# Attention logits: the product with the low part of k is given all 128 rows

## The chip, the cores and the metric

The kernel runs on one core of one Trainium2 chip. The metric is the device time of one execution in microseconds (us); lower is better. Differences of up to about 0.2% can't be told from no change with the measurements of this kernel.

## The reference, cut to what matters

The program is one block of a first network (gated linear attention, called GLA below, beside softmax attention) and two layers of a second one (softmax attention with a forget gate beside retention), all on 512 tokens of width 1024. The softmax attention of the second network, per head of 64 columns:

```
scores = jnp.einsum('bqhd,bkhd->bhqk', q_i, k).astype(jnp.float32) * scale
bias = c_i[..., :, None] - c[..., None, :]
logits = jnp.where(causal, scores + bias, -jnp.inf)
p = jax.nn.softmax(logits, axis=-1)
return jnp.einsum('bhqk,bkhd->bqhd', p.astype(v.dtype), v)
```

The first block does the same with normalized q and k and a bias by distance. Each of the three attention stages has 8 heads.

## The kernel before, in words

**Numbers in two parts.** Most matrix products run on operands of type fp32r, in which a number is held as a high part and a low part (the rest). A product of two numbers is then three products on TensorE: high with high, high with low, low with high. Activations are tiles of 128 partitions by 512 tokens; the weights come in blocks of 128x1024 through the queue of SyncE, ScalarE makes the high part of a block (wh) and VectorE the low part (wl).

**Two heads at a time.** `attention_pair` takes a PSUM tile of q and one of k, features on the partitions: head 2i on partitions 0 to 63 (in the code `r` for hh = 0), head 2i+1 on 64 to 127. For each head it makes a tile `qs`, whose half `r` is the high part of q and whose other half `x` is the low part, and a tile `kh` with the high part of k on both halves. One product over 128 partitions, `qs` with `kh`, so sums high q with high k and low q with high k. A second product on the half `r` alone, of 64 partitions, adds high q with low k (tile `kl`, shared by the two heads, one half each). The low part with the low part is left out.

**Logits.** They go by query tile t = 3, 2, 1, 0 of 128 tokens, with 512, 384 and 256 key columns (t = 1 and t = 0 share a PSUM tile of two times 256). So a head has four pairs of products, kh and then kl. VectorE adds the bias and takes the minimum (tiles ea, eb, ec, and mx for the minima), ScalarE does the exponential, VectorE scales, TensorE transposes, copies go to pta, ptb, ptc, and eight products with v give the output y of the pair, split in two by ScalarE (ymh, in the second network mixh) and VectorE (yml, mixl).

**What sets the order.** A planner in the kernel (`Weave`) interleaves threads into one order of TensorE's instructions. It holds an estimated time of TensorE and of the other engines; a thread goes on when its estimated inputs are there and PSUM banks are free by the estimate. Its cost of a product goes by the columns, not by the rows. PSUM has four banks for projections (tiles `mm`) and four for all else (tiles `at`), each taken in turn, and a product waits until the last reader of its bank is done. The order of ScalarE, VectorE and the queues is found by a scheduler when the program is built. On the chip each engine runs its own order and waits on semaphores. Projections, which have much work and need no result of the attention, fill TensorE between the steps of attention.

Names in the rows: `mm<-wh,xTh` is a projection, `at<-kh,qs` and `at<-kl,qs` the two products of the logits (first the moving operand, then the stationary one), `at<-g,u` a product of the GLA gate with 96 rows, z and cum its decays. In rows of instruction order the numbers tell tiles apart.

Of the kernel before, what the change touches and what calls it, by code (L numbers as in the profile page):

```python
# [10 lines left out]
F32 = mybir.dt.float32  # L11
# [21 lines left out]
# ---------------------------------------------------------------- weight order  # L33
def _blocks():
    """Keys (array, layer, k0, k1, c0, c1, kind) of the weight blocks."""
    out = []

    def a(name, l, c0, n, k=D, w=P):
        out.extend((name, l, 0, k, c, c + w, "") for c in range(c0, c0 + n, w))

    def b(name, l, k0, k1, c0):
        out.extend((name, l, k, k + 2 * P, c0, c0 + 512, "") for k in range(k0, k1, 2 * P))

    def low(name, l, c0, n):
        out.append((name, l, 0, D, c0, c0 + n, "low"))

    for c in (0, 512, 1024):
        b("w_in", 0, 0, D, c)
    low("w_in", 0, 3584, 16)
    a("w_in", 0, 1536, 1024)  # L50
    b("w_in", 0, 0, D, 2560)
    b("w_in", 0, 0, D, 3072)
    b("w_in", 0, 0, D, 3600)
    b("w_in", 0, 0, D, 4112)
    for i in range(4):
        for j in range(2):
            a("w_in", 0, 4624 + (2 * i + j) * P, P)
            a("w_in", 0, 5648 + (2 * i + j) * P, P)
        a("w_branch_moba", 0, 256 * i, 256, 512, 256)
        a("w_branch_gla", 0, 256 * i, 256)  # L60
    for n in range(2):
        b("w_out", 0, 0, D, 512 * n)

    def ffn(up, down, l):
        for h in range(2):
            a(up, l, 2048 * h, 2048)
            for n in range(2):
                b(down, l, 2048 * h, 2048 * (h + 1), 512 * n)

    ffn("w_up", "w_down", 0)  # L70
    for l in range(2):
        a("w_in_2", l, 0, 1024)
        low("w_in_2", l, 1536, 8)
        b("w_in_2", l, 0, D, 1024)
        a("w_in_2", l, 1544, 1024)
        b("w_in_2", l, 0, D, 2568)
        a("w_in_2", l, 3080, 512)
        for n in range(2):
            b("w_out_2", l, 0, D, 512 * n)
        ffn("w_ff1_2", "w_ff2_2", l)  # L80
    return out
# [16 lines left out]
# ---------------------------------------------------------------- constants  # L98
# [38 lines left out]
# columns of the array of per-partition vectors  # L137
# [16 lines left out]
class Event:  # L154
    """A point in the estimated time of the tensor engine."""

    t = None


class Weave:  # L160
    """Interleaves generators into one order of instructions for the tensor engine. A generator
    yields 0 to go on, or (n, event): until the event, or without one until the estimated end of
    what it gave to other engines, and until n banks of PSUM are free."""
# [10 lines left out]
    def fork(self):  # L174
        """What follows doesn't depend on the thread's earlier work on other engines."""
        self.chain = self.now
# [9 lines left out]
    def bank(self, tile):  # L186
        """A new tile takes the bank that is free first."""
        del self.banks[min(self.banks, key=self.banks.get)]
        self.banks[tile.tensor.name] = self.now
# [4 lines left out]
    def done(self):  # L194
        """The end of what the thread has given to other engines since it went on."""
        ev = Event()
        ev.t = self.ready + LAG
        return ev
# [34 lines left out]
class Engine:  # L233
    """An engine whose instructions are charged to the weave's estimate."""
# [4 lines left out]
    def book(self, start, cost):  # L239
        """The end of an instruction in the first gap from start on."""  # L240
        self.busy = [b for b in self.busy if b[1] > self.wv.now]
        t = start
        for a, b in self.busy:
            if t + cost <= a:
                break
            t = max(t, b)
        self.busy = sorted([*self.busy, (t, t + cost)])
        return t + cost
# [19 lines left out]
def model_kernel(ctx: ExitStack, tc: tile.TileContext, I, out):  # L268
# [59 lines left out]
    def split2(hi, lo, x, scale=None):  # L328
        """hi and lo of scale * x."""
        if scale is None:  # L330
            copy(hi, x)
            sub_lo(lo, x, hi)
        else:
            act.activation(hi, x, AF.Copy if isinstance(scale, float) else AF.Identity, scale=scale)
            dve.scalar_tensor_tensor(lo, x, scale, hi.bitcast(F32), ALU.mult, ALU.subtract)

    # ------------------------------------------------------------ weights
# [6 lines left out]
    def load(dst, src):  # L344
        """A load that must not run far ahead: queued behind the newest weights."""
        with tc.issue_after(last_dma[0].ins):
            nc.sync.dma_start(dst, src)
# [23 lines left out]
    class Acts:  # L371
        """K-chunks of [128, 512] as hi and lo, in groups of four or one by one."""
# [12 lines left out]
        def split(self, k, x, scale=None):  # L385
            """Chunk k = x, or scale * x with a column."""
            split2(self.hs[k], self.ls[k], x, scale)
            wv.mark(self.ev[k])

    def form_a(ps, w, c, acts, ks, toks=slice(0, T)):  # L390
        """ps[f, tok] = w[:, :, c:c+128]^T acts."""
# [9 lines left out]
    def form_b(ps, ws, acts, ks, t, first, last):  # L401
        """ps[tok, 512] += acts[:, t]^T w over blocks of two chunks."""
# [15 lines left out]
    def proj_b(name, l, k0, k1, c, acts, done, koff=0, tail=0, wait_k=False, wait_t=False, pre=None):  # L418
        """done(t, ps) as a token tile ends. The last `tail` chunks go token tile by token tile;
        pre(k) makes chunk k of acts."""  # L420
# [21 lines left out]
    # ------------------------------------------------------------ constants  # L442
# [20 lines left out]
    def rstd_col(dst, var, scale, eps):  # L463
        """dst = (var * scale + eps) ** -0.5 of up to 8 columns."""
        pool.tensor_scalar(dst, var, scale, eps, ALU.mult, ALU.add)
        pool.tensor_tensor(dst, dst, mhalf[:, 0 : dst.free_size()], ALU.pow)

    def rstd_tile(st, scale, eps, out=None):
        """(st * scale + eps) ** -0.5 of a [128, 512] PSUM tile, one Newton step after exp(-ln/2)."""
# [16 lines left out]
    def sigmoid(s, x):  # L486
        """s = 1 / (1 + exp(-x)) as exp(-ln(1 + exp(-x)))."""
        act.activation(s, x, AF.Exp, scale=-1.0)
        act.activation(s, s, AF.Ln, bias=one)
        act.activation(s, s, AF.Exp, scale=-1.0)  # L490

    def log_sigmoid(dst, t, a):
        """dst = min(t, 0) - ln(1 + exp(-|t|)); a is room."""
# [5 lines left out]
    def row_bcast(src, n0):  # L499
        """[128, 512] tile, every partition with src[n0 : n0 + 512] of a DRAM vector."""  # L500
# [4 lines left out]
    # ------------------------------------------------------------ attention with softmax  # L505
    def attention_pair(i, operands, v, bias, acts_out, done=None):
        """Softmax attention of heads 2i and 2i + 1. operands() -> PSUM tiles of q and k, [128, 512]
        feature-major, and their scales, q's negated; v[t]: [128, 512] token-major; bias(h) ->
        function t -> pieces (a, b, tile) added to the negated logits; the result goes to acts_out's
        chunk i as hi and lo."""  # L510
        qps, kps, qscale, kscale = yield from operands()
        room, ops, klo = [], [], bt("kl", F32R)
        for hh in range(2):
# [3 lines left out]
            qs, kh = bt("qs", F32R), bt("kh", F32R)  # L517
# [4 lines left out]
            ops.append((qs, kh, klo, r, bias(2 * i + hh), wv.done()))  # L522
        ec, pc2 = bt("ec"), bt("ptc")
        for hh in range(2):
            qs, kh, kl, r, pieces, ev = ops[hh]
            # probabilities by query tile t
            ea, eb = bt("ea"), bt("eb")
            es = [eb[:, 384:512], ec[:, 256 * hh : 256 * hh + 256], eb[:, 0:384], ea]
            for t in (3, 2, 1, 0):
                if t:  # L530
                    yield 1, ev
                    sx = at_ps()
                    for u in (t, 0) if t == 1 else (t,):
# [3 lines left out]
                        mm(s[:, :m], qs[r, u * P : u * P + P], kl[r, :m], False, True)  # L537
# [16 lines left out]
        # transposed by key tile  # L554
# [34 lines left out]
    # ------------------------------------------------------------ tails of a block  # L589
    def transpose_split(z, acts, t, n):  # L590
        """z: [128 tok, 512] -> chunks 4n.. of acts at tokens of t."""
# [18 lines left out]
    def add_to(res, n, alpha, part=None, then=None):  # L610
        """For proj_b: res[t][n] = alpha * res[t][n] + ps, then part(t, n) and the thread then(t)."""
# [56 lines left out]
    class LayerNorm:  # L668
        """In place over the two halves of each token tile."""
# [34 lines left out]
    # ================================================================ block 1  # L704
# [23 lines left out]
    def first_norm():  # L728
        """rstd of the first norm, as a tile over tokens and as columns."""
# [13 lines left out]
    def t5_rows():  # L743
        """T5 bias by distance, with the mask, negated, to DRAM; read back shifted by partition."""
# [21 lines left out]
    def qk_norm(dst, evs):  # L766
        """For proj_b: each head's 64 columns over their norm, without the gain."""
# [39 lines left out]
    def low_proj(w, n, acts):  # L807
        """[n, 512] product with the narrow weight columns, in SBUF."""
# [17 lines left out]
    def gla_decay(u2, g2):  # L826
        """Cumulative log decay (times 16) within chunks of 64 tokens."""
# [12 lines left out]
    def gla_head(h, gq, gk):  # L840
# [14 lines left out]
        # within a pair of chunks  # L855
# [16 lines left out]
        # over pairs: decays from the pair's start, and to its end  # L872
# [52 lines left out]
    def block1():  # L925
# [34 lines left out]
        # GLA  # L960
# [38 lines left out]
        # gates, branches  # L999
# [51 lines left out]
    # ================================================================ block 2  # L1051
# [13 lines left out]
    def ret_head(l, i, q, k, vs, decay, xi, zeta, sg, mix):  # L1065
        """Retention by chunks of 128 tokens."""
# [130 lines left out]
# ---------------------------------------------------------------- launch  # L1197
# [39 lines left out]
```

## Time and profile before

| | |
|---|---|
| median of 3 runs | 2110.65 us (2107.73 to 2112.83) |
| span of the profiled execution | 2108.8 us |
| TensorE busy | 2072.4 us, 98% of the span |
| weight loads busy | 1689.5 us, 80% |
| VectorE, ScalarE, GpSimd busy | 45%, 38%, 16% |
| mean granted TensorE clock | 0.994 of full speed |

The span runs from the first to the last instruction of the profiled execution; it lies 1.85 us under the median of the runs. A TensorE instruction is shown with a modelled end and overlaps the next, so that the distance from one start to the next, and not the duration, tells what it costs there.

### The profile page before, as it was taken

The numbers are of one execution on the slowest core, as the hardware profiler recorded it, in microseconds if no ns is written. First come the engines' busy times: TensorE is split into PE (matmuls) and PEld (weight loads), VectorE is DVE, ScalarE is ACT, GpSimd is POOL, SyncE is SP. The second block draws the span as 40 slices with busy tenths as digits, with TensorE's granted clock in tenths as the row PEclk, the third lists the DMA queues.
The fourth block names the chain that finished last, engine by engine and source line by source line (L and its number), as shares of the span: only waits on it lengthen the run. The fifth ranks groups of instructions, "written<-read, shape, count | busy, mean of one in ns | idle before, by whom it ended". The sixth has DMA issues, their size and how long they took to land.

```text
span 2108.8 us, 24494 instructions
## 1 busy us (share of the span) xinstructions
PE 2072.4 (98%) x9694; PEld 1689.5 (80%) x9694; DVE 945.2 (45%) x1602; ACT 797.4 (38%) x1237; POOL 344.0 (16%) x313
## 2 busy tenths in 40 slices
PE   8999999999999999999999999999999999999998
PEld 6777778889888888867888888888767888888886
DVE  6666444444322322475555323324674554323333
ACT  5655344333422431454334322322454334312421
POOL 2000100001300210010513300212111423201202
PEclk9999999999999999999999999999999999999999
DMA  5421112242322222322232222222322233222221
GB/s 194 151 101 60 50 65 96 100 146 81 104 100 92 98 100 80 126 90 71 80 110 90 100 91 99 100 92 78 131 85 77 74 101 104 97 100 97 93 100 40
DMA packets 62370, 202.67 MB, mean 96 GB/s; under 512 B 7278, under 2 KB 7744, under 8 KB 62256
## 3 DMA queue, kind: packets, MB, share of 16 engines
q1 hardware_dynamic: 62256, 201.12, 28.1%
q8 instruction: 76, 1.25, 0.2%
q14 instruction: 38, 0.31, 0.0%
HBM read 198.94 MB, written 4.77 MB: 97 GB/s over the span
## 4 chain that ended last, share of the span: by engine, by line
PE 94%; POOL 2%; DVE 2%; ACT 1%; issue 1%; DMA 0%; SPq 0%; POOLq 0%; ACTq 0%; DVEq 0%
PE mm L310 85%; PE at L310 7%; PE at L319 2%; POOL h L262 1%; POOL mv L262 1%; DVE h L262 0%; ACT h L262 0%; ACT sil L262 0%; DVE wl L262 0%; DMA xr<-in_xT_dram 0%; DVE og L262 0%; DVE bs L262 0%; ACT wh L262 0%; POOL gm L262 0%; DVE qs L262 0%
## 5 line engine op out<-in xcount | busy, mean ns | idle before, releaser
L262 DVE TENSOR_TENSOR wl<-wr,wh 128x1024 fp32r<-128x1024 f32 (+1 forms) x337 | 426.5, 1266 | 655.1 <-ACT wh L262 652.9
L262 ACT ACTIVATE wh<-wr 128x1024 fp32r<-128x1024 f32 (+1 forms) x340 | 358.9, 1057 | 783.1 <-PE mm L310 739.4
L310 PE MATMUL mm<-hTh,wh 128*128 128x512 f32 (+1 forms) x864 | 318.3, 368 | 0.0
L310 PE MATMUL mm<-hTl,wh 128*128 128x512 f32 (+1 forms) x864 | 317.5, 368 | 0.0
L310 PE MATMUL mm<-hTh,wl 128*128 128x512 f32 (+1 forms) x864 | 317.5, 367 | 0.0
L310 PE MATMUL mm<-wh,uh 128*128 128x512 f32 x768 | 299.2, 390 | 0.0
L310 PE MATMUL mm<-wh,ul 128*128 128x512 f32 x768 | 299.0, 389 | 0.0
L310 PE MATMUL mm<-wl,uh 128*128 128x512 f32 x768 | 298.9, 389 | 0.0
L262 POOL TENSOR_TENSOR ub<-ua 128x512 f32<-128x512 f32 x96 | 153.2, 1596 | 643.8 <-ACT ua L262 643.8
L310 PE MATMUL mm<-xTh,wh 128*128 128x512 f32 x536 | 217.9, 407 | 0.0
L310 PE MATMUL mm<-xTl,wh 128*128 128x512 f32 x536 | 209.3, 391 | 0.0
L310 PE MATMUL mm<-xTh,wl 128*128 128x512 f32 x512 | 200.2, 391 | 0.0
L310 PEld LDWEIGHTS mm<-hTh,wh 128*128 128x128 f32 x864 | 165.0, 191 | 26.1
L310 PEld LDWEIGHTS mm<-hTl,wh 128*128 128x128 f32 x864 | 164.9, 191 | 26.1
L310 PEld LDWEIGHTS mm<-hTh,wl 128*128 128x128 f32 x864 | 164.7, 191 | 26.1
L310 PEld LDWEIGHTS mm<-wh,ul 128*128 128x128 f32 x768 | 144.2, 188 | 29.9
L310 PEld LDWEIGHTS mm<-wh,uh 128*128 128x128 f32 x768 | 144.2, 188 | 29.8
L310 PEld LDWEIGHTS mm<-wl,uh 128*128 128x128 f32 x768 | 144.2, 188 | 29.8
L310 PE MATMUL mm<-wh,xTh 128*128 128x512 f32 x352 | 146.3, 416 | 11.5 <-ACT wh L262 6.0
L310 PE MATMUL mm<-wl,xTh 128*128 128x512 f32 x352 | 139.3, 396 | 0.1
L310 PE MATMUL mm<-wh,xTl 128*128 128x512 f32 x352 | 138.8, 394 | 0.5 <-DVE xTl L262 0.5
L262 DVE TENSOR_TENSOR ul<-ub,uh 128x512 fp32r<-128x512 f32 x96 | 66.5, 692 | 153.2 <-ACT uh L262 153.2
(260 smaller groups left out, 2629.2 us busy)
## 6 DMA issues: line engine op xcount, KB each, us to landing
wr<-in_wall_dram SPq DMA_DIRECT2D x338, 512.0 KB, 3.5
row<-cd SPq DMA_DIRECT2D x16, 256.0 KB, 3.8
revp<-rev SPq DMA_DIRECT2D x1, 2560.0 KB
xr<-in_xT_dram SPq DMA_DIRECT2D x8, 256.0 KB, 6.1
g<-revp SPq DMA_DIRECT2D x8, 256.0 KB, 3.9
h<-in_x_dram SPq DMA_DIRECT2D x8, 256.0 KB, 6.0
row<-in_ln_g_dram SPq DMA_DIRECT2D x8, 256.0 KB, 4.7
row<-in_ln_b_dram SPq DMA_DIRECT2D x8, 256.0 KB, 5.7
```

Of the source, the lines that this page charges most:

```text
L262: return f(out, *a, **k)
L310: nc.tensor.matmul(out, lhsT, rhs, start=start, stop=stop)
L319: nc.tensor.transpose(out, in_, ident)
```

## The change

Each head gets a `kl` tile of its own. The half `r` is written as before, and ScalarE copies it to the other half `x`, as it does for `kh`. The second product then runs over all 128 partitions, so it also adds low q with low k. The diff (comments, which it also takes out, are left away):

```diff
-        room, ops, klo = [], [], bt("kl", F32R)
+        room, ops = [], []
...
-            qs, kh = bt("qs", F32R), bt("kh", F32R)
+            qs, kh, klo = bt("qs", F32R), bt("kh", F32R), bt("kl", F32R)
...
             copy(kh[x], kh[r].bitcast(F32))
-            ops.append((qs, kh, klo, r, bias(2 * i + hh), wv.done()))
+            copy(klo[x], klo[r].bitcast(F32))
+            ops.append((qs, kh, klo, bias(2 * i + hh), wv.done()))
...
-            qs, kh, kl, r, pieces, ev = ops[hh]
+            qs, kh, kl, pieces, ev = ops[hh]
...
-                        mm(s[:, :m], qs[r, u * P : u * P + P], kl[r, :m], False, True)
+                        mm(s[:, :m], qs[:, u * P : u * P + P], kl[:, :m], False, True)
```

Since the planner books the new copy, it also puts the products in another order. Two places follow, from the first pair of the first block, and one from a later pair.

ScalarE, first pair of the first block, before: the steps of the first head (qs, kh and the copy of kh), then those of the second, and between them z of the GLA gate.

```order
L262 ACTIVATE qs_158_814<-at_155_803,gains_97 64x512 [waits PE_49]
L262 ACTIVATE kh_159_815<-at_156_804,gains_97 64x512 [waits PE_49]
L262 ACTIVATE kh_159_815<-kh_159_815 64x512 [waits Activation_49]
L262 ACTIVATE qs_161_823<-at_155_803,gains_97 64x512 [waits DVE_49]
L262 ACTIVATE kh_162_824<-at_156_804,gains_97 64x512 [waits DVE_49]
L262 ACTIVATE z_169_838<-at_168_836,cols_81 128x512 [waits PE_49]
L262 ACTIVATE kh_162_824<-kh_162_824 64x512 [waits Activation_49]
L262 ACTIVATE z_172_848<-at_171_846,cols_81 128x512 [waits PE_49]
```

The same place of the change:

```order
L262 ACTIVATE qs_157_813<-at_155_803,gains_97 64x512 [waits PE_49]
L262 ACTIVATE kh_158_814<-at_156_804,gains_97 64x512 [waits PE_49]
L262 ACTIVATE kh_158_814<-kh_158_814 64x512 [waits Activation_49]
L262 ACTIVATE kl_159_815<-kl_159_815 64x512 [waits DVE_49]
L262 ACTIVATE qs_161_824<-at_155_803,gains_97 64x512
L262 ACTIVATE kh_162_825<-at_156_804,gains_97 64x512
L262 ACTIVATE kh_162_825<-kh_162_825 64x512 [waits Activation_49]
L262 ACTIVATE z_170_841<-at_169_839,cols_81 128x512 [waits PE_49]
L262 ACTIVATE kl_163_826<-kl_163_826 64x512 [waits DVE_49]
```

The copy of kl waits for VectorE's kl of the first head and stands ahead of the second head's qs and kh, and so ahead of all that follows them.

TensorE, a little later, the second head of the same pair, before: after its product for t = 3 (not shown) there are 33 products of projections, of which the last six are shown, and then t = 2.

```order
L310 MATMUL mm_201_1006<-xTh_1_87,wh_203_1008 128x512 [waits Activation_49]
L310 MATMUL mm_201_1006<-xTl_3_89,wh_203_1008 128x512
L310 MATMUL mm_201_1006<-xTh_1_87,wl_204_1011 128x512
L310 MATMUL mm_201_1006<-xTh_1_87,wh_203_1008 128x512
L310 MATMUL mm_201_1006<-xTl_3_89,wh_203_1008 128x512
L310 MATMUL mm_201_1006<-xTh_1_87,wl_204_1011 128x512
L310 MATMUL at_205_1019<-kh_162_824,qs_161_823 128x384 [waits DVE_49]
L310 MATMUL at_205_1019<-kl_157_813,qs_161_823 128x384
```

The same head in the change:

```order
L310 MATMUL mm_147_761<-wh_182_901,xTh_2_88 128x512
L310 MATMUL mm_147_761<-wl_183_904,xTh_2_88 128x512
L310 MATMUL mm_147_761<-wh_182_901,xTl_4_90 128x512
L310 MATMUL at_193_963<-kh_162_825,qs_161_824 128x512 [waits Activation_49]
L310 MATMUL at_193_963<-kl_163_826,qs_161_824 128x512
L310 MATMUL at_195_971<-kh_162_825,qs_161_824 128x384 [waits DVE_49]
L310 MATMUL at_195_971<-kl_163_826,qs_161_824 128x384
L310 MATMUL mm_144_758<-wh_198_980,xTh_2_88 128x512
L310 MATMUL mm_144_758<-wl_199_983,xTh_2_88 128x512
```

The 33 products now stand behind t = 2, which is the fifth user of the four banks and so waits until VectorE has read the first head's t = 3.

TensorE, third pair of the first block, in the change (nine products of projections stand between the two parts, left out): the transposes of k for the fourth pair stand right ahead of the third pair's logits. Before, each pair's transposes of q and k stand behind the last transposes of the pair ahead of it.

```order
L319 MATMUL at_314_1465<-ident_91,qn_103_517 128x128
L319 MATMUL at_314_1465<-ident_91,qn_106_537 128x128
L310 MATMUL at_327_1500<-kh_293_1401,qs_292_1400 128x512 [waits DVE_49,PE_49]
L310 MATMUL at_327_1500<-kl_294_1402,qs_292_1400 128x512 [waits Activation_49]
...
L310 MATMUL at_329_1517<-kh_293_1401,qs_292_1400 128x384 [waits DVE_49]
L310 MATMUL at_329_1517<-kl_294_1402,qs_292_1400 128x384
L310 MATMUL at_331_1525<-kh_293_1401,qs_292_1400 128x256 [waits DVE_49,PE_49]
L310 MATMUL at_331_1525<-kl_294_1402,qs_292_1400 128x256
```

The product with 384 columns takes the bank of the second pair's y, and the first one with 256 columns the bank of the fourth pair's q.

## Rows read from the trace of the kernel before

**Rows 1.** The page: head, busy time, and the granted clock in 40 slices.

```profile
span 2108.8 us, 24494 instructions
...
PE 2072.4 (98%) x9694; PEld 1689.5 (80%) x9694; DVE 945.2 (45%) x1602; ACT 797.4 (38%) x1237; POOL 344.0 (16%) x313
...
PEclk9999999999999999999999999999999999999999
```

**Rows 2.** The page: chain that ended last, by engine.

```profile
PE 94%; POOL 2%; DVE 2%; ACT 1%; issue 1%; DMA 0%; SPq 0%; POOLq 0%; ACTq 0%; DVEq 0%
```

**Rows 3.** TensorE's waits: us in total, times, longest us.

```profile
PE mm L310 <- DVE qs L262: 3.4, 2, 1.7
PE at L319 <- DVE og L262: 3.0, 3, 1.6
```

**Rows 4.** Instructions that write or read kl, by form, and idle time before.

```profile
L310 PE MATMUL at<-kl,qs x96: 379/410/502, 95.0 to 1604.0; 64*128 64x256 f32 x48, 64*128 64x512 f32 x24, 64*128 64x384 f32 x24
...
  issue: 14.8, 56
```

**Rows 5.** TensorE in order of time, first logits: start, us, stationary tile, moving operand.

```profile
94.65 0.39 PE L310 MATMUL at<-kh,qs 128*128 128x512 f32 x1
94.97 0.50 PE L310 MATMUL at<-kl,qs 64*128 64x512 f32 x1
95.40 0.50 PE L310 MATMUL mm<-wh,xTh 128*128 128x512 f32 x1
95.73 0.39 PE L310 MATMUL mm<-wl,xTh 128*128 128x512 f32 x1
95.96 0.39 PE L310 MATMUL mm<-wh,xTl 128*128 128x512 f32 x1
96.18 0.33 PE L310 MATMUL at<-kh,qs 128*128 128x384 f32 x1
...
98.40 0.39 PE L310 MATMUL mm<-wl,xTh 128*128 128x512 f32 x1
```

**Rows 6.** TensorE in order of time, up-projection of the first block, 256 columns.

```profile
517.93 0.28 PE L310 MATMUL mm<-hTh,wh 128*128 128x256 f32 x1
518.05 0.28 PE L310 MATMUL mm<-hTl,wh 128*128 128x256 f32 x1
```

**Rows 7.** TensorE in order of time, a product with 96 rows.

```profile
93.73 0.39 PE L310 MATMUL at<-g,u 96*128 96x512 f32 x1
93.97 0.39 PE L310 MATMUL mm<-wh,xTh 128*128 128x512 f32 x1
```

**Rows 8.** ScalarE in order of time, first pair's operands.

```profile
89.61 0.63 ACT L262 ACTIVATE kh<-kh 64x512 fp32r<-64x512 f32 x1
90.36 0.68 ACT L262 ACTIVATE qs<-at,gains 64x512 fp32r<-64x512 f32 x1
...
91.85 0.69 ACT L262 ACTIVATE z<-at,cols 128x512 f32<-128x512 f32 x1
```

**Rows 9.** VectorE in order of time, from the first head's kl to its first minimum.

```profile
90.36 0.74 DVE L262 SCALAR_TENSOR_TENSOR kl<-at,gains,kh 64x512 fp32r<-64x512 f32 x1
91.13 0.76 DVE L262 SCALAR_TENSOR_TENSOR qs<-at,gains,qs 64x512 fp32r<-64x512 f32 x1
...
102.26 0.08 DVE L262 DVE_READ_ACCUMULATOR2_ANT mx<- 128x1 f32 x1
```

**Rows 10.** Busy time by stretch: PE, PEld, DVE, ACT, POOL.

```profile
100.00:110.00 10.00, 10.00 (x43) 7.80 (x42) 9.93 (x26) 8.08 (x18) 0.00 (x0) 1.00 0.09 25
```

**Rows 11.** Second network, TensorE: products with v, the logits behind them.

```profile
971.10 1.08 PE L310 MATMUL at<-pta,v 128*64 128x512 f32 x4
...
973.41 0.44 PE L310 MATMUL at<-kh,qs 128*128 128x384 f32 x1
```

**Rows 12.** The page: costliest groups; busy time and mean ns of one.

```profile
L262 ACT ACTIVATE wh<-wr 128x1024 fp32r<-128x1024 f32 (+1 forms) x340 | 358.9, 1057 | 783.1 <-PE mm L310 739.4
```

**Rows 13.** VectorE in order of time, low part of that y.

```profile
974.18 0.69 DVE L262 TENSOR_TENSOR mixl<-at,mixh 128x512 fp32r<-128x512 f32 x1
```

## The prediction

> **What bounds the kernel now.** I read the page first: TensorE is busy for 98% of the span at a granted clock of nine tenths or more in every slice [rows 1], and the chain that ended last lies on it for 94% [rows 2]. So a product made cheaper there shortens the run, as long as the others keep up. TensorE's waits are short; the two that touch the attention are 3.4 us for VectorE's qs and 3.0 us for og of GLA [rows 3]. None of the listed waits is of a logits product: their operands and banks were always early.
>
> Next, the instructions that touch kl [rows 4]: 96 products (3 stages x 8 heads x 4), each with a stationary tile of 64 rows where nearly all others have 128. Idle time ahead of the weight loads and products of this group has the releaser "issue", which is to say that nothing the profile shows held them.
>
> Then TensorE in order of time, by starts [rows 5]. Two projections of 512 columns with 128 rows start 0.23 us apart (95.73 and 95.96). From kh to kl it is 0.32, from kl to the projection behind it 0.43, from that to the next 0.33: 1.08 us for three products that would take 3 x 0.23 = 0.69 by the step between projections. So one 64-row product costs some 0.39 us more than its columns do: 0.09 ahead of it, 0.20 and 0.10 behind. The second cluster says the same: from 96.18 to 98.40 there are 2 products of 384 columns, 4 of 256 and one of 512, three of them kl: 2.22 us. At 0.12 us for 256 columns [rows 6], 0.17 for 384 (three quarters of 0.23) and 0.23, they would take 1.05. The excess is 1.17, again 0.39 each.
>
> Is it the fewer rows, or the other tile shape? A product with 96 rows stands in the same stretch, marked 96\*128, and the next starts 0.24 us behind it [rows 7]: no excess. It is the step between 128-row and 64-row tiles that costs, and the change takes that step away at each of the 96. That two products in a row share a stationary operand, as kh and kl do, costs nothing either: the two of [rows 6] share wh and stand 0.12 apart.
>
> **A rule that speaks against it.** The Trainium skill, TensorE: Matmul & The Clock Gate, section Why this matters for your kernels, says that a single matmul with K = 32 takes the same time as one with K = 128. By that rule alone the edit of the product would be worth 0 us here; the rows above disagree by 0.39 us a product. The Trainium skill, TensorEngine Tiling (Array Packing), section Key Properties, says that changing the tiling mode drains the TensorE, which would make the price one of the neighbours, as the rows have it.
>
> **The change, part by part.**
>
> Products: 96 x 0.39 = 37.4 us less. As bounds: nothing, if the excess had another cause than the shape; 96 x 0.42 = 40 us, with the shorter step between projections that [rows 5] also have, 0.22 (95.96 to 96.18). I take 37.4, since two clusters give the same figure. Some kl products stand next to the products with v, whose tiles have 64 columns; there one step between shapes remains, with or without the change.
>
> Copies: 24 more on ScalarE (one a head), each like the copy of kh, 0.63 us [rows 8], 15 us in all on an engine that is busy 38% [rows 1]. By themselves they lie beside TensorE. What they delay is the point. In the operands of a pair the copy stands ahead of the second head's qs and kh on ScalarE and must first wait for VectorE's kl of the first head, as the order shows.
>
> First pair of the first block, step by step. kl of the first head ends at 91.10 [rows 9], the copy then at 91.75, qs of the second head at 92.4 (before: 90.36 + 0.68 = 91.04 [rows 8]). VectorE's half of qs, 0.76 us long, then ends at 93.2 and not at 91.89 [rows 9]. The third GLA gate product takes the bank of that q and stood at 92.1 without a wait, so it waits about 1.2 us. Behind the second head's kh and its copy comes z: ScalarE reaches its end at about 94.4, where before it was 91.85 + 0.69 = 92.54 [rows 8]. VectorE's decays of GLA begin with that z and run on up to the first head's minimum, read at 102.26 to 102.34; VectorE is full there, 9.93 of 10 us [rows 10]. So this minimum comes some 1.9 us later, at 104.2. The change has the second head's t = 2 ahead of the 33 projections, not behind; it takes the bank of just that tile. TensorE would be there at 94.65 + 1.2 + 6.5 = 102.4 (two products each of 512, 384; four of 256; 21 projections; again two of 512, at the steps above), and waits 1.8 us. Together 3.0 us; bounds 0 (VectorE catches up) and 5.
>
> Third pair of the first block. Behind its transposes TensorE does 3 projections (0.7), the second pair's products with v (2.3, from 971.10 to 973.41 in [rows 11]) and 6 projections (1.4), the fourth pair's transposes (0.9), two logits products (0.5) and 9 projections (2.1), at 7.9 us from the start. ScalarE meanwhile has, in the order of the change, eight operand steps, one weight block, two GLA tiles and then ymh: at the durations of [rows 8] and 1.06 us for the block [rows 12] that ends about 7.9, and VectorE's yml 0.7 later; the fourth pair's qs, kh, copy and second qs follow, and VectorE's half of that at 11.2. The product with 384 columns waits for yml, the one with 256 for this qs: together about 3 us; bounds 0 and 5.
>
> GLA, first block: the waits for og [rows 3] fall where a head's output is normalized. In the change three more GLA products of 256 columns stand in front of the first of these transposes; I take 1 us off the 1.6 us wait. Bounds: 2 us gained, 3 lost.
>
> Second network, two layers. Three times a layer logits follow right on the products with v, and one of them takes the bank of y. With 64-row products it came late enough. Now it is there about 1.3 us after the products with v, while y's low part ends at 974.87 against 973.41, 1.46 us after them [rows 11, 13], more if VectorE is busy: 0.3 us each. The wait for qs [rows 3] is the rv projection waiting for the last pair's bank; the copy ahead of the second head's qs adds some 0.4 us, and a transpose that follows the logits closely some 0.3. That is 2 x (0.9 + 0.4 + 0.3) = 3.2 us; bounds 0 and 8.
>
> The sum: -37.4 + 3.0 + 3 - 1 + 3.2 = -29.2 us. Against the profiled span, 2108.8, it gives 2079.6; the median of the runs is 1.85 above that span, so the median becomes 2081.4 us, 1.4% less.
>
> **Rivals.**
>
> *The time comes back as waits.* ScalarE has more to do where it is busiest, VectorE is full at 100 to 110 us [rows 10], and the faster TensorE asks for banks earlier. If VectorE's chain sets the pace in half of the time, the gain halves: 37.4 / 2 - 4 (the first block's waits beyond those counted) is 15, time 2096. Against it: the planner has projections to put in between, and blocks of weights lie ready. I give it 0.15.
>
> *The waits don't come.* If the schedulers' order leaves room where I count waits, only the price stands: 2110.65 - 38 = 2072.5 or less. 0.10.
>
> *Slower.* The excess could belong to the order of products (logits between projections) and not to the tile's shape; then kl to the next start stays at 0.43 us for 512 columns, nothing is gained, and the rest of the sum, 3.0 + 3 - 1 + 3.2 = 8.2 us, remains: 2119. It decides on the step from kl to the next product: the waits win if less than 8.2 / 37.4 = 0.22 of the price goes, that is if the step stays above 0.43 - 0.22 x 0.20 = 0.39 us. Against it stand [rows 7] and [rows 6]. 0.04. By the rule on K above this is the case that would come.
>
> *No change.* The same with part of the gain, 7 to 12 us, which the waits eat: 0.03.
>
> **How the numbers follow.** My forecast, 2074 to 2090 us, has 0.68; the waits' rival 0.15; no waits 0.10; slower 0.04; no change 0.03. The range 2072 to 2094 takes the forecast, most of no waits and a third of the first rival, some 0.8. A measurement here can tell 0.2%, 4.2 us, from no change: faster 0.93, same 0.03, slower 0.04.
>
> **What the profile after would show.** kl as 128\*128 with 96 records; starts from kl to the next product 0.23 us apart for 512 columns, 0.12 for 256; idle time by "issue" ahead of this group near nothing. 24 copies of kl of 0.63 us. Waits of TensorE in logits products for VectorE (mx, qs, yml, mixl), a few us in all, and one of about 1 us of a GLA gate product near 92 us. Weight blocks no later than before. I am wrong if the step between kl and its neighbours stays, or if the waits of logits and transposes exceed some 15 us.

## The result and the profile after

The change takes 2085.84 us (median of 4 runs, 2082.91 to 2087.82) where the kernel before, in the same session, takes 2110.49: 0.9883 of it, with a 95% interval of 0.9869 to 0.9897. That is 24.65 us or 1.2% less; 29.2 were forecast. The profiled executions differ by 24.9 us (2108.8 and 2083.9).

The page of the change, busy time and chain, answers to [rows 1, 2]:

```profile
PE 2037.8 (98%) x9694; PEld 1685.6 (81%) x9694; DVE 939.8 (45%) x1602; ACT 808.5 (39%) x1261; POOL 342.7 (16%) x313
...
PE 92%; DVE 2%; ACT 2%; POOL 2%; issue 1%; DMA 0%; POOLq 0%; ACTq 0%; DVEq 0%; SPq 0%
```

TensorE does the same 9694 products in 34.6 us less busy time. The span fell by only 24.9, so some 10 us of new idle time must stand on TensorE; the chain shows the same, 92% on it instead of 94%.

The instructions that touch kl, by form, and who waits for whom (answers to [rows 4]):

```profile
L310 PE MATMUL at<-kl,qs x96: 277/309/398, 94.7 to 1580.7; 128*128 128x256 f32 x48, 128*128 128x512 f32 x24, 128*128 128x384 f32 x24
L262 ACT ACTIVATE kl<-kl x24: 612/630/632, 89.6 to 1552.4; 64x512 fp32r<-64x512 f32 x24
...
  ACT kl L262: 9.9, 16
```

The 96 products have 128 rows, the idle time by "issue" (14.8 us in [rows 4]) is gone, and there are 24 copies of 0.63 us on ScalarE. New is the last line: in 16 of the 24 ScalarE stood still, 9.9 us in all, until VectorE's kl was there.

TensorE in order of time, first block (start, us, stationary tile, moving operand; idle time and its releaser in brackets):

```profile
91.84 0.47 PE L310 MATMUL at<-g,u 96*128 96x512 f32 x1 [1.12 <-DVE qs L262]
...
94.47 0.39 PE L310 MATMUL at<-kh,qs 128*128 128x512 f32 x1
94.69 0.39 PE L310 MATMUL at<-kl,qs 128*128 128x512 f32 x1
94.92 0.39 PE L310 MATMUL mm<-wh,xTh 128*128 128x512 f32 x1
95.15 0.39 PE L310 MATMUL mm<-wl,xTh 128*128 128x512 f32 x1
...
102.72 0.44 PE L310 MATMUL at<-kh,qs 128*128 128x384 f32 x1 [1.55 <-DVE mx L262]
...
158.31 0.35 PE L310 MATMUL at<-kh,qs 128*128 128x256 f32 x1 [1.94 <-DVE qs L262]
```

From kh to the second product behind kl it is 95.15 - 94.47 = 0.68 us, where [rows 5] have 95.73 - 94.65 = 1.08: the price of 0.40 is gone. The rows in brackets are the waits that came in its place.

TensorE's waits, in total, times and longest (answers to [rows 3]):

```profile
PE at L310 <- DVE sta L262: 6.5, 4, 4.1
PE mm L310 <- DVE qs L262: 5.9, 2, 2.9
...
PE at L310 <- DVE qs L262: 3.1, 2, 1.9
...
PE at L310 <- ACT pta L262: 1.7, 2, 0.9
PE at L310 <- DVE mx L262: 1.6, 1, 1.6
PE at L319 <- DVE og L262: 1.4, 2, 1.0
...
PE at L310 <- DVE yml L262: 0.2, 1, 0.2
```

Before, qs ahead of projections stood at 3.4 and og at 3.0 [rows 3], sta at 2.9:

```profile
PE at L310 <- DVE sta L262: 2.9, 4, 1.4
```

The other four were not in the list. The difference is 3.6 + 2.5 + 3.1 + 1.7 + 1.6 + 0.2 - 1.6 = 11.1 us. Two waits of before are gone, for ScalarE's xTh (1.3) and VectorE's sil (0.8); 9.0 us remain, which is about the gap between busy time and span (34.6 - 24.9 = 9.7).

Where it comes from is seen best where the projection rv of the second network waits for the last pair's bank. The chain that ended last, layer 0 of the second network (start, us, what):

```profile
932.77 0.69 DVE kl L262
...
933.49 0.63 ACT kl L262
...
934.13 0.60 ACT qs L262
...
934.75 0.70 DVE qs L262
...
935.50 1.44 PE mm L310 x3
```

Read it from the top: VectorE's low part of the first head's k; the copy of that kl on ScalarE, which can't start earlier; only then the second head's qs on ScalarE, which stands behind the copy; its low part on VectorE; and the projection, which needs that bank. Nothing in the arithmetic makes the second head's qs depend on the first head's kl. The order of one engine does.

### The profile page after: what moved, and what is told of

The parts are those of the page before. It is cut to its first block, busy times and chain, and to the rows that moved or that the text cites. A ratio compares the mean times of both kernels' runs of the same rounds, so it can differ in the third digit from the quotient of the medians.

```text
span 2083.9 us, 24530 instructions
## 1 busy us (share of the span) xinstructions
PE 2037.8 (98%) x9694; PEld 1685.6 (81%) x9694; DVE 939.8 (45%) x1602; ACT 808.5 (39%) x1261; POOL 342.7 (16%) x313
## 3 DMA queue, kind: packets, MB, share of 16 engines
q8 instruction: 76, 1.25, 0.2%
## 4 chain that ended last, share of the span: by engine, by line
PE 92%; DVE 2%; ACT 2%; POOL 2%; issue 1%; DMA 0%; POOLq 0%; ACTq 0%; DVEq 0%; SPq 0%
PE mm L310 84%; PE at L310 5%; PE at L319 2%; POOL h L262 1%; POOL mv L262 1%; ACT wh L262 0%; DVE wl L262 0%; DVE h L262 0%; ACT h L262 0%; ACT kh L262 0%; DVE og L262 0%; ACT qs L262 0%; DVE qs L262 0%; ACT sil L262 0%; DVE bs L262 0%
## 5 line engine op out<-in xcount | busy, mean ns | idle before, releaser
L310 PE MATMUL mm<-wh,xTh 128*128 128x512 f32 x352 | 145.4, 413 | 12.5 <-ACT wh L262 6.5
```

Source lines behind the costliest of these rows:

```text
L310: nc.tensor.matmul(out, lhsT, rhs, start=start, stop=stop)
```

## Experiments

Each ran beside the kernel before, whose median was 2110.53 us for the first four and 2109.17 for the last three. Ratios are to it, with 95% intervals.

**Product back on 64 rows (e1_rows64).** The change with one edit:

```diff
-mm(s[:, :m], qs[:, u * P : u * P + P], kl[:, :m], False, True)
+mm(s[:, :m], qs[64 * hh : 64 * hh + 64, u * P : u * P + P], kl[64 * hh : 64 * hh + 64, :m], False, True)
```

> The changed kernel with its copies of kl and its order of products, but the second product on 64 rows again, so the copied halves are not used. Theory: the price of 0.39 us lies in the step between 128-row and 64-row tiles. Then 96 x 0.39 = 37 us come back, less what they hide of the changed kernel's waits (some 6 us): 2113 to 2123 us, slower than the kernel before, with starts 0.43 us apart from kl to a projection. Rival: the gain came from the new order of the products; then this stays at 2083 to 2089 us.

Measured 2126.71 us, ratio 1.0073 (1.0058 to 1.0089). TensorE in order of time at the first logits:

```profile
95.08 0.39 PE L310 MATMUL at<-kh,qs 128*128 128x512 f32 x1
95.40 0.50 PE L310 MATMUL at<-kl,qs 64*128 64x512 f32 x1
95.83 0.50 PE L310 MATMUL mm<-wh,xTh 128*128 128x512 f32 x1
96.16 0.39 PE L310 MATMUL mm<-wl,xTh 128*128 128x512 f32 x1
```

1.08 us again (95.08 to 96.16), and slower than before, as the theory has it; but 3.7 us above the range that was expected. With the same copies and the same order, the way back to 64 rows costs 2126.71 - 2085.84 = 40.9 us, or 0.43 a product. Not all of it is the price of the products: the mean granted clock of the profiled execution is 0.989 here and 0.994 in the change, and 0.011 x 2125.7 - 0.006 x 2083.9 is some 11 us of full speed. That leaves some 30 us, 0.31 a product, and the wait for mx (1.6 us in the change) is gone here, hidden by the slower products. Copies and order without the wide product cost 16 us against the kernel before (clock 0.994); by the same count some 11 of these are clock too. Why the clock fell more here is open.

**Two 64-row products side by side (e2_grouped).** The kernel before; where t = 1 and t = 0 share a PSUM tile, the second pair is turned round, so that the two kl are neighbours:

```diff
-                        mm(s[:, :m], qs[:, u * P : u * P + P], kh[:, :m], True, False)
-                        mm(s[:, :m], qs[r, u * P : u * P + P], kl[r, :m], False, True)
+                        two = [(qs, kh, slice(0, P)), (qs, kl, r)]
+                        for n, (a, b, rows) in enumerate(two if u else two[::-1]):
+                            mm(s[:, :m], a[rows, u * P : u * P + P], b[rows, :m], n == 0, n == 1)
```

> The kernel before with one edit: for t = 0 the kl product goes first and the kh product second, so that the kl products of t = 1 and t = 0 stand side by side and 24 of the 96 steps into and out of 64-row tiles go, with no other change of work. Theory (the step costs): 24 x 0.39 = 9.4 us less, 2101 us. Rival (a 64-row product is slow by itself): 2110 us, within 2 us of before.

Measured 2099.37 us, ratio 0.9946 (0.9931 to 0.9961). TensorE in order of time:

```profile
97.08 0.38 PE L310 MATMUL at<-kh,qs 128*128 128x256 f32 x1
97.39 0.50 PE L310 MATMUL at<-kl,qs 64*128 64x256 f32 x2
97.82 0.39 PE L310 MATMUL at<-kh,qs 128*128 128x256 f32 x1
98.05 0.40 PE L310 MATMUL mm<-wh,xTh 128*128 128x512 f32 x1
```

The row marked x2 is both kl. Not one product got more rows here, and 11.2 us went: 24 pairs of steps between shapes fewer, 0.47 each (0.34 to 0.61 by the interval). So what costs is the step from one tile shape to the other and back, not the 64 rows themselves. What stands still at the step shows in TensorE's weight loads (start, us), of the first kl of the kernel before and of the change:

```profile
94.97 0.18 PEld L310 LDWEIGHTS at<-kl,qs 64*128 64x128 f32 x1 [0.35 <-issue]
...
94.47 0.19 PEld L310 LDWEIGHTS at<-kl,qs 128*128 128x128 f32 x1
```

Before, the load of the 64-row tile starts only with its own product (94.97 in [rows 5]), after 0.35 us in which the loads stood still. In the change it starts 0.22 us ahead of its product (94.69), while the product of kh runs. This is the idle time by "issue" of [rows 4].

**The copy in the old order, and zeros in its place (e5_copy_unbooked, e6_zeros_unbooked).** In both the planner isn't told of the new step, and TensorE's order is that of the kernel before. The first keeps the copy on ScalarE, the second has GpSimd write zeros to the other half of kl (it leaves out the term low q with low k, as the kernel before does):

```diff
-            copy(klo[x], klo[r].bitcast(F32))
+            nc.scalar.activation(klo[x], klo[r].bitcast(F32), AF.Copy)   # first
+            nc.gpsimd.memset(klo[x].bitcast(F32), 0.0)                   # second
```

> The changed kernel, but the planner is not told of the copy of kl, so that TensorE has the order of before. Theory A: the waits that ate a third of the gain came from the planner's new order (GLA heads side by side, t = 2 ahead of the projections, transposes ahead of logits); then only the last pair's bank costs more than before, and the time is 2076 to 2080 us. Theory B: the copy on ScalarE makes them in any order, since it holds back the second head's operands; then 2084 to 2090 us.

> The other half of kl is set to zero by GpSimd, not booked in the planner, instead of being copied by ScalarE; the second product runs on 128 rows and adds what it added before. TensorE has the order of before, and nothing waits for VectorE's kl. Both theories of the waits: only the price is left, 96 x 0.39 = 37 us less than before, 2072 to 2075 us. Rival: a faster TensorE runs into waits that no copy makes; then 2078 us or more.

Measured 2084.21 us with the copy, ratio 0.9867 (0.9851 to 0.9884), and 2072.44 with zeros, 0.9820 (0.9805 to 0.9834). With the copy this is theory B, not A. TensorE's waits are then, in the old order:

```profile
PE mm L310 <- DVE qs L262: 5.9, 2, 2.9
...
PE at L319 <- DVE og L262: 3.0, 3, 1.7
PE at L310 <- DVE sta L262: 2.9, 4, 1.4
...
PE at L310 <- ACT pta L262: 1.6, 2, 0.8
PE mm L310 <- ACT v L262: 1.6, 1, 1.6
PE at L310 <- DVE qs L262: 1.1, 1, 1.1
PE at L310 <- DVE yml L262: 1.0, 1, 1.0
```

og and sta are back at their old figures, so the long wait for sta in the change needs the planner's new order. But by the medians the sum doesn't care: the copy makes other waits (v, yml) here, and the time is that of the change within what can be told. With zeros 38.1 us go by the medians, 0.40 a product, and 35.7 by the profiled executions (2108.8 and 2073.1). TensorE's order is the same in both, so the starts can be compared one by one: the kl products and their neighbours, away from waits and from the lower clock, are 36.6 us closer together, 0.38 a product. Each of TensorE's waits is within 0.3 us of what it was before: nothing comes back.

**Work or wait (e7_scalar_zeros).** ScalarE again has 24 steps at the same place (a few in the first block lie one or two steps off), but from the high part of k times 0, which it has just written itself:

```diff
-            copy(klo[x], klo[r].bitcast(F32))
+            nc.scalar.activation(klo[x], kh[r].bitcast(F32), AF.Copy, scale=0.0)
```

> The changed kernel, but ScalarE writes zeros to the other half of kl (the high part of k times 0) where the change has the copy, at the same place in its order, and the planner isn't told, so that TensorE's order is that of the kernel before. ScalarE's work is the same 24 steps of 0.63 us, but none of them waits for VectorE's kl. The term with the low part of q is left out, as in the kernel before. Theory (the copy costs because it stands waiting for VectorE's kl ahead of the second head's operands): most of the 11.8 us between the unbooked copy, 2084.2, and the zeros by GpSimd, 2072.4, is won back: 2073 to 2079. Rival (it is ScalarE's 15 us of work, whatever it waits for): 2081 to 2086.

Measured 2075.04 us, ratio 0.9837 (0.9822 to 0.9851). The chain ahead of the same rv projection, and then ScalarE's group:

```profile
925.87 0.68 DVE kl L262
...
926.59 0.70 DVE qs L262
```

```profile
L522 ACT ACTIVATE kl<-kh 64x512 fp32r<-64x512 f32 x24 | 14.7, 614 | 0.0
```

ScalarE does the same work (14.7 us) without one wait, and VectorE goes from kl to the second qs 0.03 us later, without the 0.63 + 0.60 us on ScalarE between them in the change. Most of the loss is gone: 9.2 us less by the medians, 6.3 by the ratios. The work itself is left with some 2.6 us over zeros by GpSimd (3.6 by the ratios), which the intervals don't tell from nothing; TensorE's list has short waits for pta (0.8) and yml (0.6) that it doesn't have with GpSimd's zeros.

**The same numbers without ScalarE (e8_copy_gpsimd).** GpSimd copies:

```diff
-            copy(klo[x], klo[r].bitcast(F32))
+            nc.gpsimd.tensor_copy(klo[x], klo[r].bitcast(F32))
```

> The changed kernel, with the copy of kl made by GpSimd in place of ScalarE and not told to the planner, so that TensorE's order is that of the kernel before; the same numbers are computed as in the change. Theory (the copy hurts only by what it holds back on ScalarE): as with zeros by GpSimd, 2072 to 2077. Rival 1 (the products need the copied half itself so early that they wait for it): 2080 to 2086, with waits of logits products for GpSimd's kl. Rival 2 (GpSimd's copies slow VectorE's steps down, or hold back GpSimd's own work): 2078 to 2084, with VectorE's operands longer or later.

Measured 2071.15 us, ratio 0.9818 (0.9803 to 0.9832): it computes what the change computes, some 14 us faster (13.7 by the ratios, 14.7 by the medians), and a little under the range expected. Against the copy on ScalarE in the same order of TensorE's products it is 10.3 by the ratios and 13.1 by the medians. GpSimd's group, and then TensorE's waits:

```profile
L522 POOL CAST kl<-kl 64x512 fp32r<-64x512 f32 x24 | 18.7, 780 | 327.7 <-DVE kl L262 276.5 <-issue 41.2 <-DVE mx L262 9.8
```

```profile
PE mm L310 <- DVE qs L262: 3.4, 2, 1.7
PE at L319 <- DVE og L262: 3.0, 3, 1.7
PE at L310 <- DVE sta L262: 2.9, 4, 1.4
```

GpSimd sat 276.5 us in front of these copies until VectorE's kl came, far longer than ScalarE's 9.9, and it cost nothing: what is queued behind there is early. No product waits for the copied half, and the three waits are those of before. Both rivals fell.

**Zeros, booked (e3_zeros).** The planner is told of GpSimd's zeros and makes a third order:

```diff
-            copy(klo[x], klo[r].bitcast(F32))
+            pool.memset(klo[x].bitcast(F32), 0.0)
```

> Zeros by GpSimd in the other half of kl as in the best run so far, 2072.4, but booked with the planner, so that TensorE's order changes (416 rows differ from that of the kernel before). ScalarE has no copy. The term with the low part of q is left out, as in the kernel before. If a new order of the planner costs nothing by itself: 2071 to 2075. If orders that the planner makes with more work booked run into bank waits of their own: 2076 to 2082.

Measured 2071.62 us, ratio 0.9821 (0.9805 to 0.9837), as with the old order. This third order costs nothing by itself. The order of the change was not run without the copy, so what it costs alone is not shown.

**Where the time goes, by stretches.** Marks are starts of TensorE instructions: the last transposes of og (end of the first block's attention and GLA) and the first product of the retention in each layer (`at<-ra,ra`). Each figure is the stretch's length minus that of the kernel before, in us; the first stretch is counted from the first `at<-oh,t`, which stands ahead of everything changed (76.25 before, 74.69 in the change). So 1.6 of the 24.9 us stand ahead of everything changed; with the copy in the old order that start is at 77.91, 3.2 us later than in the change, and spans that are equal hide this.

| | to the last og | to ra, layer 0 | to ra, layer 1 |
|---|---|---|---|
| forecast, 32 products less the waits | -7.5 | -10.9 | -10.9 |
| the change | -4.7 | -7.9 | -10.1 |
| copy, old order | -9.6 | -8.5 | -9.3 |
| ScalarE's zeros | -10.6 | -11.8 | -12.6 |
| GpSimd's zeros | -12.2 | -12.2 | -12.7 |
| GpSimd's copy | -13.4 | -12.3 | -12.8 |

Without the copy on ScalarE each stretch gives 11 to 13 us, about the price of 32 x 0.39 = 12.5. With it each is short, in either order; in the order of the change the first stretch gains 4.9 us less than in the old one.

## Why the prediction held, and where it didn't

**The price: right.** 37.4 us were forecast; 36.6 came by the starts with zeros in the old order and 38.1 by the medians, so that 38.1 lies this near is in part luck. The 40.9 between the two kernels of the new order have some 11 us of clock in them. That it is the step between shapes and not the rows is shown by the pair side by side. The rival in which the price belongs to the order of products is out: from kl to the next start it is now 0.23 us, not 0.43. The Trainium skill, TensorE: Matmul & The Clock Gate, section Why this matters for your kernels, by whose rule the rows change nothing, doesn't cover this: a lone product among products of another shape pays 0.4 us for its neighbours.

**That the copy's place on ScalarE brings waits: right in kind.** Gate product 1.2 us forecast, 1.12 measured; t = 2 on the minimum 1.8 and 1.55; third pair 3 and 0.21 + 1.94. These three were followed row by row through the engines in the prediction.

**What was mis-sized: the GLA and rv terms.** The waits were put at 8.2 us net, and 9.0 came; but they are other ones in part, and that the sums are so near is luck. First pair and third pair came to 4.8 us (6.0 forecast), GLA to 2.0 lost (1 gained), the second network to 4.2 (3.2), and 2.1 went with xTh and sil, which weren't forecast to move. Busy time fell by 34.6 us and not by 37.4; where the rest is, is open. The granted clock doesn't explain it: its mean is 0.994 in both kernels.
- *GLA, "I take 1 us off".* The wait for og fell by 1.6, but sta rose by 3.6. The chain shows how:

```profile
216.45 1.05 POOL gm L262
...
217.53 1.66 DVE og L262 x4
219.19 0.34 DVE sta L262
...
219.57 2.08 PE at L310 x4
```

VectorE's copy of sta stands behind four scalings of og, which wait for GpSimd's gm; TensorE, there early, waits 4.13 us. The old order doesn't have this with the same copy (1.4 at most), and in the new order with 64-row products it is there too (4.1): it takes the new order. Whether the order would do it without the copy no run shows. It was read as a gain by looking at one wait (og) and not at what else VectorE had queued behind og.
- *rv projection, "some 0.4 us".* It is 2.94 us in each layer where [rows 3] have 1.7: 1.25 more. The estimate took the copy as a slight delay; in fact the second head's qs is put behind VectorE's kl, and so 0.63 for the copy and 0.60 for that qs both stand between two steps of VectorE that the chain of before has 0.03 apart:

```profile
944.30 0.68 DVE kl L262
...
945.01 0.70 DVE qs L262
```

- *The bank of y and the transposes, 0.3 each.* No wait for mixl is in the list. In their place came one of 0.85 us a layer for ScalarE's pta.

**The loss, divided.** From the best versions, 2071 to 2072, to the change, 2085.8, it is some 14 us. By the medians 9.2 (6.3 by the ratios) are the copy's wait on ScalarE; its work is 2.6 (3.6) and the new order 1.6 (3.4); the last two are too small to be told from nothing. By the stretches of the table, one profiled execution each and without the start, the wait is 7.6, the work 2.1 and the order 4.7. So the wait is the largest part by each count, and how the rest divides stays open. The rival "the time comes back as waits" had the right mechanism, at about a third of the price instead of half.

**Open.** Why the clock falls behind one wait and not behind another (below), why it fell more with 64 rows in the new order (0.989 against 0.994), and what the new order costs without the copy.

## What to carry to other kernels

A lone product of another tile shape among equal ones costs by its two steps; fill the missing rows (zeros do), or put products of one shape side by side. Before a step is added to an engine, ask what it waits for and what stands behind it in that engine's order: with TensorE's order the same, the copy cost 10 to 13 us less on GpSimd, which waited far longer but held nothing up. And when a wait is forecast to shrink, look at what else its engine has queued behind that same event.

## What the hardware showed that was not expected

Behind two of the longer waits the granted clock fell to its lower level, 1.2 GHz. Stretches of the change (busy us of PE, PEld, DVE, ACT, POOL, then the granted clock):

```profile
218.00:222.00 4.00, 2.42 (x6) 1.98 (x7) 2.31 (x7) 0.00 (x0) 0.00 (x0) 0.62 0.00 0
222.00:226.00 4.00, 4.00 (x16) 3.27 (x15) 0.92 (x2) 1.31 (x3) 0.00 (x0) 0.52 0.00 0
...
936.00:938.00 2.00, 2.00 (x7) 1.53 (x6) 1.29 (x3) 0.63 (x1) 2.00 (x2) 0.50 0.00 0
938.00:941.00 3.00, 3.00 (x17) 2.46 (x15) 0.00 (x0) 0.77 (x2) 0.42 (x1) 0.80 0.00 0
...
1552.00:1554.00 2.00, 2.00 (x11) 1.60 (x10) 1.39 (x3) 0.70 (x2) 1.87 (x2) 1.00 0.01 5
```

The first two are behind the wait of 4.13 us for sta: at 0.62 and 0.52 some 0.38 x 4 + 0.48 x 4 = 3.4 us of full speed are lost. (The kernel before has a smaller fall at the same place in GLA, 0.81 and 0.76 from 222 to 230 us, which is 1.7.) The others are behind the same rv projection in the two layers, each after a wait of 2.94 us: in layer 0 the clock is at half, with 512-column products 0.43 us apart (935.88 and 936.31) and not 0.23, which loses 1.0 + 0.2 x 3 = 1.6 us; in layer 1 it is whole. So behind a wait more can be lost than its own length, and the length alone doesn't say whether it is. That the wait brings the fall is not shown either: with GpSimd's zeros in the old order and with GpSimd's copy the transposes of og wait 1.65 us alike (up to 212.50 and 210.75 us), and from 210 to 220 us the clock is 0.83 in the one and 1.00 in the other. Nor do these falls explain why the change gained less than forecast. The kernel before loses more later, near its waits of 2.6 us for GpSimd's h: 0.83 from 1110 to 1130 us and 0.67 from 1740 to 1750, some 6.7 us of full speed, where the change has 0.83 from 1100 to 1110 and from 1720 to 1730, some 3.4.
